# An encoder layer in emulated float32: 60 stores begun by GpSimd and 16 by ScalarE instead of SyncE

## The chip, the cores and the metric

The kernel runs on one core of a Trainium2 chip. Its time is device microseconds (us) of one execution, and of several runs the median is given. The engines are named as the profile names them: PE (TensorE, matrix products), DVE (VectorE), ACT (ScalarE), POOL (GpSimd) and SP (SyncE, which here only begins transfers). Each engine works through its own instructions in a fixed order. An instruction that begins a transfer (a DMA) stands in that order too: whatever it waits for, the instructions behind it on the same engine wait as well.

## The reference

One layer over 1024 frames of 1024 channels, all in float32. A product with `w_in` gives queries, keys, values, gates and merge logits. Branch A is a chunked gated linear attention, branch B a pooling mixer; the merged rows go through `w_out` and a layer norm.

```python
h = x @ w_in
q, k, v, gate_a, alpha_low, pool_in, gate_b, merge_logits = jnp.split(h, IN_OFFSETS, axis=-1)
...
y_a = o.reshape(B, S, GLA_DV).astype(x.dtype) * jax.nn.silu(gate_a)
y_b = _multiscale_pool(pool_in, w_pool_grp, pool_scale).astype(x.dtype) * jax.nn.silu(gate_b)
gates = jax.nn.sigmoid(merge_logits + b_merge)
g_a, g_b = jnp.split(gates, N_BRANCHES, axis=-1)
merged = g_a * (y_a @ w_proj_a) + g_b * (y_b @ w_proj_b)
y = merged @ w_out
return _layernorm(DEEPNORM_ALPHA * x + y, ln_g, ln_b)
```

## The kernel before

PE multiplies in float32 by parts: each operand is split into a high and a low part (L52, an ACT cast; L53, a DVE subtraction), and three products of the parts are summed.

Up to about 380 us the kernel loads `x`, projects, and runs the four attention heads; eight rows `la` (merge logits of branch A) are made in between by `la_gen`, copied by ACT and stored to DRAM (`la_d`, L295). From then on the work consists of pairs of output rows, each pair a 2 x 2 block product done with seven products instead of eight, of twelve matmuls each. The pairs, in order: `pi0..3` and `gb0..3` (branch B's input and gate), `gta0..3` (gate of branch A), `lb0..3` (merge logits of branch B), `pb0..3` (projection of branch B), `pa0..3` (projection of branch A, and the merge), `o0..3` (`w_out`).

Of a pair's seven weight blocks three are quarters of the raw weights (`raw_lb` and the like, L675) and four are sums of quarters, `S7`, `S6`, `S5`, `S3` (L614). POOL forms these sums for `pi`, `gb`, `gta` and `lb`, DVE for the later pairs. A product can't start before its sum has been formed and split.

The other operand of a product needs sums as well: four differences of its quarters, `T1..T4`. They are formed ahead of time: `Operands.ahead` loads four pieces (`xp`, `ybp`, `wop`, `yap`), POOL forms four 128x1024 differences (L196), and each is stored to DRAM (L198) and read back when its stage comes (L208). This is done twice for each of the operands X (at 29 to 56 us), YB (hooked to `gta0`, `gta1`), WO (`gta2`, `gta3`) and YA (`lb0`, `lb1`).

In `pb` and `pa` the product's rows are multiplied by a gate row (L835, L838/L839) and, in `pa`, added to the stored row of `pb` (L841). L839 and L841 run on POOL (in `pa3` on DVE). The results are stored by halves: `mb_d` (L851, 16 stores) and `m_d` (L855, 12 stores). The sigmoid rows of `lb` are stored to `gb_d` (L810, 8 stores) and read back as gates of `pb`.

All transfers of the kernel before, loads and stores, are begun by SP, on one hardware queue. A scheduler fixes each engine's order when the kernel is built, so moving a store to another engine also shifts other rows; the order is the same in every run.

Of the kernel before, what the change touches and what calls it, by code (L numbers as in the profile page):

```python
# [35 lines left out]
def encoder_layer(ctx: ExitStack, tc: tile.TileContext, xT, x, w_av, w_v, w_blk, w_up, b_al, g_norm,  # L36
                  w_pool, p_scale, b_mrg, w_pa, w_pb, w_o, ln_g, ln_b, ident_c, rcnt_c, masks_c, out):
    nc = tc.nc
    act, dve, pool_e, pe, sp = nc.scalar, nc.vector, nc.gpsimd, nc.tensor, nc.sync
# [73 lines left out]
    def w_in_gen(j, nm, then):  # L113

        w = load_split(w_blk[j], (KB, P), nm)
        ps = ps_acc.tile([P, S], F32, tag="acc", name=f"ps_{nm}")
        for half in range(2):
            i = 0
            for k in range(KB):
                hi, lo = w(k)  # L120
                for a, b in ((hi, xq[0]), (hi, xq[1]), (lo, xq[0])):
                    pe.matmul(ps[:, half * 512:half * 512 + 512], lhsT=a, rhs=mov(b, k, half), start=(i == 0), stop=(i == 23))  # L122
                    i += 1
                    yield 216
        then(ps)
# [58 lines left out]
    class Operands:  # L184
# [3 lines left out]
        def ahead(self, g, piece):  # L188

            q = {}  # L190
            for n in ("22", "12", "11", "21"):
                q[n] = piece(n, f"{self.nm}p{n}_{g}")
                self.fetch(q[n], n, g)
            for o, out_, a, b, op in (("T3", "22", "22", "12", ALU.subtract), ("T1", "12", "12", "11", ALU.subtract),
                                      ("T2", "11", "22", "11", ALU.add), ("T4", "21", "21", "11", ALU.subtract)):
                pool_e.tensor_tensor(out=q[out_], in0=q[a], in1=q[b], op=op)  # L196
                self.td[o, g] = dram.tile([P, 2, 512], F32, name=f"{self.nm}{o}_{g}d", tag=f"{self.nm}{o}_{g}d")
                sp.dma_start(self.td[o, g], q[out_])  # L198

        def make(self, o, pool):  # L200

# [50 lines left out]
    la_d = [dram.tile([P, S], F32, name=f"la_{j}", tag=f"la_{j}") for j in range(KB)]  # L252
# [38 lines left out]
    def la_gen(j, pool):  # L291
        def then(ps):
            s = pool.tile([P, S], F32, tag="sg", name=f"la_{j}")
            act.copy(s, ps)
            sp.dma_start(la_d[j], s)  # L295
        return w_in_gen(32 + j, f"la{j}", then)

    def ends(h):
# [275 lines left out]
    hs_ = (slice(0, 512), slice(512, 1024))  # L574

    def row(nm):
        return c4.tile([P, S], F32, tag="c", name=nm)
# [96 lines left out]
    def blk(w, j0):  # L674
        return lambda t, i: sp.dma_start(t.rearrange("p (a b) -> p a b", a=KB), w[j0 + i])  # L675
# [15 lines left out]
    def d_tile(nm):  # L691
        return dram.tile([P, S], F32, name=nm, tag=nm)

    yb_d, ya_d = Kept("yb"), Kept("ya")
    YB, YA = Operands("yb", yb_d.get), Operands("ya", ya_d.get)
    gb_d = [d_tile(f"gb_{j}") for j in range(KB)]
    mb_d = [d_tile(f"mb_{j}") for j in range(KB)]
    m_d = [dram.tile([P, 4, S], F32, name="m_0", tag="m_0"), dram.tile([P, 2, S], F32, name="m_1", tag="m_1")]
# [4 lines left out]
    def change(old, new):  # L703

        names = [p[1] for p in PRODUCTS]
        hooks = {0: [lambda: new.make("B11", op_a), lambda: new.make(names[1], old.pool[names[0]])]}
        for i in range(1, 6):
            hooks[i] = [lambda i=i: new.make(names[i + 1], old.pool[names[i]])]
        return hooks
# [80 lines left out]
    def y_a(j0):  # L790
# [10 lines left out]
        return then  # L801

    more = [ahead(YB, 0), ahead(YB, 1), ahead(WO, 0), ahead(WO, 1)]
    for q in range(4):
        items.append(gate_pair(f"gta{q}", 8 + 2 * q, AF.Silu, y_a(2 * q), hooks=more[q]))

    def keep(j0):
        def then(t):
            for i in range(2):
                sp.dma_start(gb_d[j0 + i], t(i))  # L810
        return then

    more = [ahead(YA, 0), ahead(YA, 1), None, change(X, YB)]
    for q in range(4):
        items.append(gate_pair(f"lb{q}", 40 + 2 * q, AF.Sigmoid, keep(2 * q), bias=8 + 2 * q, hooks=more[q]))


    def gated(nm, j0, operands, w, gate, more_d, out, hooks, eng):
        g, mb = {}, {}

        def get(i):
            if i not in g:
                g[i] = row(f"g{nm}_{i}")
                with tc.high_priority(offset=150):
                    gate(g[i], j0 + i)
                if more_d:
                    mb[i] = row(f"mb{nm}_{i}")
                    with tc.high_priority(offset=150):
                        sp.dma_start(mb[i], more_d[j0 + i])
            return g[i]  # L830

        def use(i, half, ps, more):
            o = get(i)[:, hs_[half]]
            if more is None:
                dve.tensor_tensor(out=o, in0=ps, in1=o, op=ALU.mult)  # L835
            else:
                t = post.tile([P, 512], F32, tag="t", name=f"t{nm}_{i}{half}", bufs=2)
                dve.tensor_tensor(out=t, in0=ps, in1=more, op=ALU.add)  # L838
                eng.tensor_tensor(out=o, in0=t, in1=o, op=ALU.mult)  # L839
            if more_d:  # L840
                eng.tensor_tensor(out=o, in0=o, in1=mb[i][:, hs_[half]], op=ALU.add)  # L841
            out(j0 + i, half, o)
        return Pair(nm, blk(w, j0), operands, use, hooks=hooks, s_eng=dve), get

    def gate_a(t, j):
# [2 lines left out]

    for q in range(4):
        items.append(gated(f"pb{q}", 2 * q, YB, w_pb, lambda t, j: sp.dma_start(t, gb_d[j]), None,  # L850
                           lambda j, half, o: sp.dma_start(mb_d[j][:, hs_[half]], o), change(YB, YA) if q == 3 else None, pool_e)[0])  # L851
    for q in range(4):
        def to_dram(j, half, o):
            if j < 6:
                sp.dma_start(m_d[j // 4][:, j % 4, hs_[half]], o)  # L855
        pair, m_last = gated(f"pa{q}", 2 * q, YA, w_pa, gate_a, mb_d, to_dram, change(YA, WO) if q == 3 else None,
                             dve if q == 3 else pool_e)
        items.append(pair)
# [136 lines left out]
```

## Time and profile before

| | us |
|---|---|
| median of 3 runs (1007.59 to 1009.13) | 1008.87 |
| the profiled execution | 1003.91 |
| its span in the trace | 1002.1 |
| PE busy in the span | 942.5 (94%) |
| DVE / ACT / POOL busy | 761.3 / 386.1 / 359.5 |
| moved by the one DMA queue | 163.59 MB |

The span is what the trace covers; the profiled execution is 1.8 us longer than its span and 4.96 us (0.5%) below the median of the runs. "PE" counts matmuls, "PEclk" is the clock that the throttle granted to PE as a share of full speed. A releaser ("<-") is the instruction whose end let a waiting instruction go.

### The profile page before, as it was taken

The numbers are of one execution on the slowest core, as the hardware profiler recorded it, in microseconds if no ns is written. First come the engines' busy times: TensorE is split into PE (matmuls) and PEld (weight loads), VectorE is DVE, ScalarE is ACT, GpSimd is POOL, SyncE is SP. The second block draws the span as 40 slices with busy tenths as digits, with TensorE's granted clock in tenths as the row PEclk, the third lists the DMA queues.
The fourth block names the chain that finished last, engine by engine and source line by source line (L and its number), as shares of the span: only waits on it lengthen the run. The fifth ranks groups of instructions, "written<-read, shape, count | busy, mean of one in ns | idle before, by whom it ended". The sixth has DMA issues, their size and how long they took to land. (4 is left out here: it accounts for less than half of the span.)

```text
span 1002.1 us, 13009 instructions
## 1 busy us (share of the span) xinstructions
PE 942.5 (94%) x4744; PEld 758.5 (76%) x4744; DVE 761.3 (76%) x1036; ACT 386.1 (39%) x625; POOL 359.5 (36%) x193
## 2 busy tenths in 40 slices
PE   9999799998999998999999999899999998989992
PEld 6887797886886885888888887678888876766871
DVE  5359959869666256857787778788886896689997
ACT  5255244253241225434333333233752552353330
POOL 1525323213213022322224267779111245510653
PEclk9999999999999999999999999999999999998997
DMA  8921120331123246121312498998987584496232
GB/s 274 348 85 34 40 74 22 76 111 42 44 91 84 85 121 230 43 95 53 118 52 94 136 331 305 325 330 325 385 287 250 215 323 162 165 302 200 102 120 84
DMA packets 72400, 164.41 MB, mean 164 GB/s; under 512 B 10208, under 2 KB 26848, under 8 KB 72336
## 3 DMA queue, kind: packets, MB, share of 16 engines
q1 hardware_dynamic: 72336, 163.59, 47.3%
q8 instruction: 37, 0.61, 0.3%
q14 instruction: 27, 0.22, 0.1%
HBM read 114.28 MB, written 49.28 MB: 163 GB/s over the span
## 5 line engine op out<-in xcount | busy, mean ns | idle before, releaser
L391 POOL TENSOR_TENSOR ks<-k,e 128x1024 f32<-128x1024 f32 x20 | 57.5, 2882 | 77.1 <-ACT e L387 67.5
L839 POOL TENSOR_TENSOR gpb<-tpb,gpb 128x512 f32<-128x512 f32 x12 | 21.6, 1799 | 87.5 <-DVE tpb L838 72.8
L122 PE MATMUL ps_la<-xh,wlo_la 128*128 128x512 f32 x128 | 51.4, 402 | 0.0
L122 PE MATMUL ps_la<-xl,whi_la 128*128 128x512 f32 x128 | 51.4, 401 | 0.0
L122 PE MATMUL ps_la<-xh,whi_la 128*128 128x512 f32 x128 | 51.0, 398 | 0.0
L387 ACT ACTIVATE e<-e 128x1024 f32<-128x1024 f32 x20 | 21.1, 1060 | 49.4 <-DVE e L386 49.3
L453 POOL TENSOR_TENSOR rsr_o<-rsa_o,mhalf 128x8 f32<-128x8 f32 x4 | 6.6, 1646 | 89.9 <-DVE rsa_o L452 89.9
L140 PE MATMUL ps_v<-whi_v,xh 128*128 128x264 f32 x128 | 37.4, 294 | 1.3 <-DVE k L288 1.3
L140 PE MATMUL ps_v<-whi_v,xl 128*128 128x264 f32 x128 | 37.5, 294 | 0.0
L444 DVE COPY v<-ps_o 128x256 f32<-128x256 f32 x32 | 13.4, 421 | 31.5 <-PE ps_o L441 25.6
L140 PE MATMUL ps_v<-wlo_v,xh 128*128 128x264 f32 x128 | 37.3, 294 | 0.0
L320 POOL TENSOR_TENSOR ke<-k,e 128x1024 f32<-128x1024 f32 x4 | 12.0, 3011 | 58.0 <-DVE k L288 28.6
L402 PEld LDWEIGHTS ps_s<-qs,ks 128*64 128x64 f32 x640 | 22.5, 140 | 13.7 <-issue 13.2
L390 DVE TENSOR_TENSOR qs<-q,e 128x1024 f32<-128x1024 f32 x20 | 30.2, 1512 | 3.2 <-ACT e L387 3.2
L614 POOL TENSOR_TENSOR S_gb<-raw_gb,raw_gb 128x512 f32<-128x512 f32 x4 | 6.3, 1587 | 67.1 <-DMA raw_gb<-in_w_blk 51.6
L402 PE MATMUL ps_s<-qs,ks 128*64 128x64 f32 x640 | 26.7, 229 | 3.3 <-DVE Pc L406 1.7
L122 PEld LDWEIGHTS ps_la<-xh,whi_la 128*128 128x128 f32 x128 | 24.2, 189 | 5.8 <-issue 0.4
L122 PEld LDWEIGHTS ps_la<-xl,whi_la 128*128 128x128 f32 x128 | 24.2, 189 | 5.4
L122 PEld LDWEIGHTS ps_la<-xh,wlo_la 128*128 128x128 f32 x128 | 24.2, 189 | 5.3
L196 POOL TENSOR_TENSOR ybp<-ybp,ybp 128x1024 f32<-128x1024 f32 x8 | 21.8, 2730 | 15.2 <-DMA ybp<-yb 10.6
L445 ACT ACTIVATE ps_o<-v 128x256 f32<-128x256 f32 x32 | 12.4, 387 | 37.5 <-DVE v L444 37.5
L122 PE MATMUL ps_k<-xl,whi_k 128*128 128x512 f32 x64 | 26.7, 417 | 0.0
(585 smaller groups left out, 3324.1 us busy)
## 6 DMA issues: line engine op xcount, KB each, us to landing
raw_v<-in_w_v SPq DMA_DIRECT2D x16, 264.0 KB, 2.7
xp<-in_xT SPq DMA_DIRECT2D x8, 512.0 KB, 6.7
oT<-oTs SPq DMA_DIRECT2D x32, 128.0 KB, 2.5
raw_la<-in_w_blk SPq DMA_DIRECT2D x8, 512.0 KB, 3.9
la<-la SPq DMA_DIRECT2D x8, 512.0 KB, 5.2
raw_pi<-in_w_blk SPq DMA_DIRECT2D x8, 512.0 KB, 4.3
raw_gb<-in_w_blk SPq DMA_DIRECT2D x8, 512.0 KB, 3.6
yb<-gb SPq DMA_DIRECT2D x16, 256.0 KB, 2.1
```

The costliest lines, as they stand in the source:

```text
L122: pe.matmul(ps[:, half * 512:half * 512 + 512], lhsT=a, rhs=mov(b, k, half), start=(i == 0), stop=(i == 23))
L140: pe.matmul(o, lhsT=sta(a, k, tb), rhs=w(k - k0)[b], start=(k == 0 and i == 0), stop=(k == KB - 1 and i == 2))
L196: pool_e.tensor_tensor(out=q[out_], in0=q[a], in1=q[b], op=op)
L320: pool_e.tensor_tensor(out=ke, in0=k, in1=e1, op=ALU.mult)
L387: act.activation(e, e, AF.Exp, scale=1.0 / TAU)
L390: dve.tensor_tensor(out=qs, in0=qt[h], in1=e, op=ALU.mult)
L391: pool_e.tensor_tensor(out=ks, in0=kt_[h], in1=e, op=ALU.mult)
L402: pe.matmul(psv[c * CH:c * CH + CH, b, :], lhsT=ks[:, cs], rhs=qs[:, cs], start=True, stop=True)
L444: dve.tensor_copy(v[b][:, hs], po)
L445: act.activation(po, v[b][:, hs], AF.Square, accum_out=d["ss"][:, b:b + 1])
L453: pool_e.tensor_tensor(out=r, in0=a, in1=mhalf[:, :w], op=ALU.pow)
L839: eng.tensor_tensor(out=o, in0=t, in1=o, op=ALU.mult)
```

## The change

76 stores are begun by another engine than SP: the 32 stores of differences (L198), the 16 of `mb` (L851) and the 12 of `m` (L855) by POOL, the 8 of `la` (L295) and the 8 of `gb` (L810) by ACT. Each stands in its new engine's order behind the instruction that makes its data, except that one half in four of `mb` is finished by DVE (L835): there POOL's store waits for DVE. The rows of `pa3` are stored neither before nor now. The number of bytes moved is the same. SP keeps all loads and the stores of `yb`, `ya` (L686), `oT` and `out`. SP's rows go from 377 to 302, POOL's from 198 to 258, ACT's from 590 to 606.

```diff
@@ Operands.ahead
                 pool_e.tensor_tensor(out=q[out_], in0=q[a], in1=q[b], op=op)
...
-                sp.dma_start(self.td[o, g], q[out_])
+                pool_e.dma_start(self.td[o, g], q[out_])
@@ la_gen
             act.copy(s, ps)
-            sp.dma_start(la_d[j], s)
+            act.dma_start(la_d[j], s)
@@ keep
-                sp.dma_start(gb_d[j0 + i], t(i))
+                act.dma_start(gb_d[j0 + i], t(i))
@@ gated
-            out(j0 + i, half, o)
+            out(j0 + i, half, o, pool_e if eng is pool_e else sp)
@@ pb
-                           lambda j, half, o: sp.dma_start(mb_d[j][:, hs_[half]], o), change(YB, YA) if q == 3 else None, pool_e)[0])
+                           lambda j, half, o, q: q.dma_start(mb_d[j][:, hs_[half]], o), change(YB, YA) if q == 3 else None, pool_e)[0])
@@ pa
-        def to_dram(j, half, o):
+        def to_dram(j, half, o, q):
             if j < 6:
-                sp.dma_start(m_d[j // 4][:, j % 4, hs_[half]], o)
+                q.dma_start(m_d[j // 4][:, j % 4, hs_[half]], o)
```

The first place is POOL's order around the weight sums of `lb1`, at some 657 to 680 us of the trace before. `S_lb_5538`, `5558`, `5580` and `5658` are S7, S6, S5 and S3 of `lb1`; `yap_0` are the four pieces of YA's first half. Before:

```order
L614 TENSOR_TENSOR S_lb_5538<-raw_lb_0_5344,raw_lb_1_5346 128x512
L614 TENSOR_TENSOR S_lb_5558<-raw_lb_1_5346,S_lb_5538 128x512
L614 TENSOR_TENSOR S_lb_5580<-raw_lb_1_5346 128x512
L614 TENSOR_TENSOR S_lb_5658<-raw_lb_0_5344,S_lb_5558 128x512
L196 TENSOR_TENSOR yap_0_5437<-yap_0_5437,yap_0_5439 128x1024
L196 TENSOR_TENSOR yap_0_5439<-yap_0_5439,yap_0_5441 128x1024
L196 TENSOR_TENSOR yap_0_5441<-yap_0_5437,yap_0_5441 128x1024
L196 TENSOR_TENSOR yap_0_5443<-yap_0_5443,yap_0_5441 128x1024
```

The same place of POOL's order in the changed kernel:

```order
L196 TENSOR_TENSOR yap_0_5437<-yap_0_5437,yap_0_5439 128x1024
L198 DMA yaT_0d<-yap_0_5437 128x1024
L196 TENSOR_TENSOR yap_0_5439<-yap_0_5439,yap_0_5441 128x1024
L198 DMA yaT_0d<-yap_0_5439 128x1024
L196 TENSOR_TENSOR yap_0_5441<-yap_0_5437,yap_0_5441 128x1024
L614 TENSOR_TENSOR S_lb_5538<-raw_lb_0_5344,raw_lb_1_5346 128x512
L198 DMA yaT_0d<-yap_0_5441 128x1024
L196 TENSOR_TENSOR yap_0_5443<-yap_0_5443,yap_0_5441 128x1024
L614 TENSOR_TENSOR S_lb_5558<-raw_lb_1_5346,S_lb_5538 128x512
L614 TENSOR_TENSOR S_lb_5580<-raw_lb_1_5346 128x512
L198 DMA yaT_0d<-yap_0_5443 128x1024
L614 TENSOR_TENSOR S_lb_5658<-raw_lb_0_5344,S_lb_5558 128x512
```

Three differences and two stores have moved ahead of S7 of `lb1`, and the fourth difference and the other two stores stand between its four sums. The orders around the sums of `gta2`, `lb0` and `lb2` change in the same way.

The second place is SP's order in the `pa` stage, at some 824 to 842 us, as one piece of the difference ("-" before, "+" after). `raw_pa_1_6865` is the second half of a pair's weights, `gpa` and `mbpa` are rows read for the merge, `m_3238` is where merged rows are stored.

```order
 L829 DMA mbpa_0_7047<-mb_3232 128x1024
-L855 DMA m_3238<-gpa_1_6853 128x512
-L855 DMA m_3238<-gpa_0_6883 128x512
-L855 DMA m_3238<-gpa_1_6853 128x512
 L846 DMA gpa_1_7175<-la_521 128x1024
+L675 DMA raw_pa_1_6865<-in_w_pa 128x1024
 L829 DMA mbpa_1_7178<-mb_3235 128x1024
-L675 DMA raw_pa_1_6865<-in_w_pa 128x1024
-L855 DMA m_3238<-gpa_0_6883 128x512
 L846 DMA gpa_0_7205<-la_520 128x1024
```

The weights' second half no longer stands behind three stores of merged rows, and it has changed places with the load of `mbpa`.

## Rows read from the trace of the kernel before

**Rows 1.** The page's first part: busy time, share of the span, instructions.

```profile
PE 942.5 (94%) x4744; PEld 758.5 (76%) x4744; DVE 761.3 (76%) x1036; ACT 386.1 (39%) x625; POOL 359.5 (36%) x193
```

**Rows 2.** Busy time by stretch (window: its length, each engine, PEclk, DMA share, GB/s).

```profile
575.00:600.00 25.00, 25.00 (x110) 20.27 (x109) 17.29 (x18) 9.48 (x16) 16.66 (x10) 1.00 0.89 314
600.00:625.00 25.00, 23.82 (x103) 18.86 (x102) 21.88 (x19) 9.95 (x17) 19.94 (x11) 1.00 0.81 305
625.00:650.00 25.00, 20.81 (x83) 16.43 (x82) 18.62 (x14) 6.64 (x12) 19.04 (x10) 0.93 0.93 330
650.00:675.00 25.00, 23.66 (x102) 18.93 (x101) 21.69 (x15) 10.38 (x16) 19.37 (x10) 1.00 0.94 344
675.00:700.00 25.00, 25.00 (x109) 20.23 (x108) 21.65 (x18) 8.62 (x14) 24.61 (x12) 1.00 0.85 306
```

**Rows 3.** Timeline of PE, matmuls that waited (start, duration, [idle before <-releaser]).

```profile
613.60 0.50 PE L635 MATMUL psa_gta<-xh,wlo_gta 128*128 128x512 f32 x1 [1.18 <-DVE wlo_gta L53]
...
640.01 0.71 PE L635 MATMUL psc_gta<-xT4h,whi_gta 128*128 128x512 f32 x1 [4.19 <-DVE e_gta L644]
...
844.45 0.47 PE L635 MATMUL psc_pa<-yaT4h,whi_pa 128*128 128x512 f32 x1 [3.15 <-DVE e_pa L644]
...
901.88 0.79 PE L635 MATMUL psc_o<-woT3h,whi_o 128*128 128x512 f32 x1 [4.32 <-ACT whi_o L52]
```

**Rows 4.** Busy time by stretch, behind the third of these waits.

```profile
844.90:848.30 3.40, 3.40 (x10) 2.63 (x9) 3.37 (x5) 0.40 (x1) 2.59 (x2) 0.50 0.00 1
```

**Rows 5.** Waits of SP's queue (line <- releaser: us in total, times, longest).

```profile
SPq L855 <- POOL gpa L841: 30.5, 8, 6.8
...
SPq L851 <- POOL gpb L839: 25.7, 10, 7.5
...
SPq L198 <- POOL ybp L196: 18.6, 7, 6.3
...
SPq L295 <- ACT la L294: 7.0, 1, 7.0
```

**Rows 6.** Groups by shape on POOL (busy us, mean ns of one | idle before).

```profile
L196 POOL TENSOR_TENSOR yap<-yap,yap 128x1024 f32<-128x1024 f32 x8 | 22.2, 2780 | 0.4
...
L841 POOL TENSOR_TENSOR gpa<-gpa,mbpa 128x512 f32<-128x512 f32 x12 | 19.6, 1644 | 0.7
...
L614 POOL TENSOR_TENSOR S_lb<-raw_lb,S_lb 128x512 f32<-128x512 f32 x8 | 11.4, 1429 | 6.9 <-DVE wlo_lb L53 6.6
...
L614 POOL TENSOR_TENSOR S_lb<-raw_lb,raw_lb 128x512 f32<-128x512 f32 x4 | 7.0, 1755 | 2.0 <-DMA raw_lb<-in_w_blk 2.0
...
L614 POOL TENSOR_TENSOR S_lb<-raw_lb 128x512 f32<-128x512 f32 x4 | 6.0, 1507 | 0.6 <-DVE wlo_lb L53 0.6
...
L453 POOL TENSOR_TENSOR rsr_ln<-rsa_ln,mhalf 128x1 f32<-128x1 f32 x8 | 4.9, 613 | 12.5 <-DVE rsa_ln L452 9.9 <-DVE rst_ln L456 2.6
```

**Rows 7.** Timeline of POOL, 657 to 684 us (a difference is wop or yap).

```profile
657.40 2.27 POOL L614 TENSOR_TENSOR S_lb<-raw_lb,raw_lb 128x512 f32<-128x512 f32 x1
659.74 1.63 POOL L614 TENSOR_TENSOR S_lb<-raw_lb,S_lb 128x512 f32<-128x512 f32 x1
...
667.88 1.29 POOL L614 TENSOR_TENSOR S_lb<-raw_lb,S_lb 128x512 f32<-128x512 f32 x1 [4.61 <-DVE wlo_lb L53]
669.12 14.11 POOL L196 TENSOR_TENSOR yap<-yap,yap 128x1024 f32<-128x1024 f32 x5
```

**Rows 8.** The chain that ended last, at the product of `lb1` with S7.

```profile
671.27 2.78 PE psc_lb L635 x12
```

**Rows 9.** Timeline of SP, 825 to 834 us (start, duration, what it begins).

```profile
825.14 6.14 SPq L855 DMA_DIRECT2D m<-gpa  x2
831.33 0.42 SPq L846 DMA_DIRECT2D gpa<-la  x1
833.38 0.32 SPq L829 DMA_DIRECT2D mbpa<-mb  x1
833.79 0.38 SPq L675 DMA_DIRECT2D raw_pa<-in_w_pa  x1
```

## The prediction, made before the changed kernel ran

> **What bounds the kernel now.** I read the page's busy times first: PE works in 94% of the span, and no other engine comes near [rows 1]. What can be won is therefore only time in which PE waits or runs at the lower clock, and what can be lost is new waiting of PE. Next I read the busy times in stretches of 25 us around the stage where POOL forms differences for three operands while it also forms the weight sums [rows 2]. PE is full in the first and the last of these stretches and lacks 1.18, 4.19 and 1.34 us in the three between; POOL lacks 8.34, 5.06, 5.96, 5.63 and 0.39 us of 25, together 25.4 us of 125. This is the only stage where POOL is nearly as full as PE, and it is where 24 of the 60 stores that POOL receives will be issued (YB's, WO's and YA's, eight each). Then the timeline of PE for its largest waits [rows 3]: each is released by DVE or ACT, which themselves follow a late load or a late row. The two larger ones behind 800 us are where SP's order matters. [...] Last, the waits of SP's queue [rows 5]: it stands 30.5 us for merged rows (L855), 25.7 for `mb` (L851), 18.6 for YB's differences and 7.0 for the one late `la` row, with later loads queued behind it.
>
> **What the change adds on POOL.** No transfer is begun by POOL in this trace, so its price there, d, is unknown. From below, the shortest arithmetic on POOL takes 0.61 us; from above, a 128x512 operation takes 1.64 [rows 6]. SP's own issues take 0.32 to 0.42 [rows 9], but I see no reason why POOL should match them, and use 0.61 as the low end. I take 1.0, as far from the one as from the other in ratio. Besides, an instruction that needs the result of the one ahead of it on POOL starts 0.07 us behind it (659.74 after 657.40 + 2.27) [rows 7], so a store costs 1.07.
>
> A pair of rows keeps PE busy for 7 products of 2.78, 19.46 us [rows 8]. In a pair with differences POOL does four of 2.78 (11.12) and four sums, 1.755 + 2 x 1.429 + 1.507 = 6.12, together 17.24 [rows 6], which leaves 2.22. Four stores at 1.07 are 4.28, so each such pair leaves POOL 2.06 us further behind. All 24 stores are 25.7 us, about the 25.4 that POOL has idle, and not all of that idle time can be used, since part of it waits for DVE, as the 4.61 us ahead of 667.88 do [rows 7].
>
> This alone would be absorbed, since sums are formed early. S7 of `lb1` ends at 659.67, PE needs its product at 671.27: a lead of 11.60 [rows 7, 8]. But the new order places three differences and two stores ahead of that S7: 3 x 2.78 + 2 x 1.07 = 10.48. The lead that is left is 1.12. POOL arrives there with the lateness of the three pairs `gta2`, `gta3` and `lb0`, 3 x 2.06 = 6.18, so S7 comes 6.18 - 1.12 = 5.06 late. The cover that hid POOL's work is then gone, and the rest of `lb1` and `lb2`, each with four stores, add 2.06 each, 4.12. Late sums make ACT's and DVE's splits late, and PE waits for these. One such wait will be long enough to be followed by the lower clock: 1.7 [rows 4]. **Loss: 5.06 + 4.12 + 1.7 = 10.9 us.** At d = 0.61 a pair is late by 0.50 and S7 isn't late (lead 1.9 against 1.5): about 1.0. At d = 1.64 a pair is late by 4.62, S7 by 14.0, and the loss is 14.0 + 9.2 + 1.7 = 25. Where the wait of 4.19 us at 640.01 stays, POOL catches up there; where DVE's new order removes it, PE gains as much. I count neither.
>
> The eight stores of X (29 to 56 us) and those of `mb` and `m` lie where POOL has room: it is busy for 36% of the span [rows 1]. I cost them at nothing; their cover is POOL's idle time, and if POOL became late in `pa`, its 12 rows would free `mbpa` later by one store each and the loads behind them too.
>
> [...]
>
> **What it gives on SP.** In `pa` SP stands until 831.28 for two stores of merged rows, and the weights' second half goes out at 833.79, behind the load of `mbpa` [rows 9]. In the new order it stands behind the load of `gpa` alone: 831.4 instead of 833.79, 2.4 us earlier. The wait at 844.45 becomes 3.15 - 2.4 = 0.75, short enough, as at 613.60, to be followed by no lower clock: gain 2.4 + 1.7 = 4.1. The wait of 4.32 at 901.88 follows `w_out` loads that stood behind merged rows in SP's queue; POOL's rows get later there too, so I take half, 2.2, between 0 and 4.32. The store of `la` that held SP for 7.0 us stood ahead of loads for `pi`; up to 1 us, counted in the low end alone. **Gain: 6.3 us,** at most 9.4.
>
> **What it adds on ACT.** Sixteen issues; by SP's rows 0.32 to 0.42 each [rows 9], at most 6.7 us on an engine that is busy for 39% [rows 1]. What hides them is ACT's idle time. If a `gb` store has to wait for an earlier transfer, the casts of weights queue behind it; I give that nothing in the sum.
>
> **Sum.** 10.9 - 6.3 = +4.6 us. The profiled execution took 1003.91, so 1008.5 for its like. It lies 4.96 below the median of the runs, and against that the same difference gives 1008.87 + 4.6 = 1013.5.
>
> **Rivals.**
> 1. *POOL has room after all.* If d is 0.6 or less, the loss is 1 us or none and SP's gain remains: -5.3 to -9.4, 1003.6 to 999.5. For it: 24 x 0.68 = 16.3 us against 25.4 idle. It decides from about d = 0.77 down: there a pair is late by 1.14, the lead left at S7 is 1.58, and the loss, 3 x 1.14 - 1.58 + 2 x 1.14 = 4.1 without a lower clock, is 2.2 below the gain. Against it: three differences ahead of a sum, whatever d is. 36%.
> 2. *Nothing to be seen.* The loads that go out earlier land no earlier, since the DMA engines are 81 to 94% busy at 575 to 700 us [rows 2], and POOL's lateness is covered by waits that PE has anyway (6.7 us in the three middle stretches). Both terms shrink to a few us: 1007 to 1011. 16%.
> 3. *Stores on POOL are dear.* If a store is held for as long as POOL's own operations beside DVE, d is 1.64, the loss 25 and the time 1008.87 + 18.7 = 1027.6. For it: DVE is busy 17 to 22 of 25 us there [rows 2]. 10%. [...]
>
> **Chances and range.** The forecast, a loss of a few us with d near 1, has 38%, and its own range is 1011 to 1019. A measurement of this kernel can tell about 0.2%, 2 us, from no change. Slower by more: forecast and third rival, 48%. Within: the second, 16%. Faster: the first, 36%. The range goes from the first rival's full gain, 999, to 1025, short of the dear case.
>
> **What would show it.** Right: POOL is full from 600 to 700 us; stores there take about 1 us of its order; PE waits for `wlo_lb` or `whi_lb` behind S7 at some 670 us; the wait at 844 shrinks to below 1 us without a lower clock. Wrong: PE as full at 600 to 700 us as before, POOL with idle time left (first rival), or a new wait of ACT on a `gb` store. What would make the sum wrong most easily is d, and next the loads: if YA's pieces land late, POOL waits for them ahead of S7, and the loss grows without any price of a store.

## The result, and the profile after

The changed kernel took 1029.60 us (median of 4 runs, 1025.02 to 1033.84) against 1008.27 for the kernel before on the same chip: ratio 1.0232 on record (the medians alone give 1.0212), 95% interval 1.0204 to 1.0261. It is slower by 21 us, beyond the predicted range. The profiled execution is the slowest of the four, 1033.84 us with a span of 1031.8, while that of the kernel before lay 4 to 5 us below its median. So the two spans differ by 29.7 us, and losses read from the two traces are together some 8 us larger than the 21 us of the medians.

Up to the pair `gta1` the two traces keep step: it starts at 581.15 us before and at 581.49 after. `lb3` starts at 707.29 and at 738.99. Of this stretch, 31.4 us longer, one row of the kernel before, by stretch as in [rows 2]:

```profile
581.15:707.29 126.14, 119.43 (x506) 95.65 (x504) 99.94 (x81) 45.78 (x74) 99.25 (x48) 0.99 0.90 329
```

and one of the changed kernel:

```profile
581.49:738.99 157.50, 131.64 (x506) 103.94 (x505) 109.70 (x81) 45.34 (x75) 100.26 (x71) 0.89 0.75 272
...
600.00:625.00 25.00, 20.82 (x79) 16.50 (x78) 19.04 (x15) 6.83 (x13) 14.06 (x11) 0.84 0.80 281
...
650.00:675.00 25.00, 19.97 (x77) 15.74 (x76) 21.04 (x13) 6.87 (x12) 15.78 (x12) 0.86 0.66 235
```

PE does the same 506 matmuls. It idles 157.50 - 131.64 = 25.86 us instead of 6.71, and the same work takes 12.2 us longer at a mean granted clock of 0.89 instead of 0.99. The last two rows answer to the second and fourth of [rows 2]: POOL, which the prediction saw full here, is busy for 14 and 16 of 25 us, less than before. The waits of PE that make up 21.7 of the 25.86 us, from the timeline of PE after (they answer to [rows 3]):

```profile
613.43 0.80 PE L635 MATMUL psc_gta<-xT3h,wlo_gta 128*128 128x512 f32 x1 [4.18 <-DVE wlo_gta L53]
...
639.40 0.79 PE L635 MATMUL psc_gta<-xT3h,wlo_gta 128*128 128x512 f32 x1 [4.09 <-DVE wlo_gta L53]
...
664.11 0.80 PE L635 MATMUL psa_lb<-xh,wlo_lb 128*128 128x512 f32 x1 [5.03 <-DVE wlo_lb L53]
...
693.49 0.79 PE L635 MATMUL psc_lb<-xT3h,wlo_lb 128*128 128x512 f32 x1 [3.00 <-DVE wlo_lb L53]
...
711.26 0.76 PE L635 MATMUL psc_lb<-xT4h,whi_lb 128*128 128x512 f32 x1 [5.36 <-DVE e_lb L644]
```

All five end with DVE. What DVE did is read from its timeline after:

```profile
605.19 8.18 DVE L53 TENSOR_TENSOR wlo_gta<-S_gta,whi_gta 128x512 fp32r<-128x512 f32 x1 [3.44 <-ACT whi_gta L52]
613.30 0.68 DVE L759 TENSOR_TENSOR gta<-psc_gta,u_gta 128x512 f32<-128x512 f32 x1
...
631.24 8.11 DVE L53 TENSOR_TENSOR wlo_gta<-S_gta,whi_gta 128x512 fp32r<-128x512 f32 x1 [1.21 <-ACT whi_gta L52]
...
651.72 12.33 DVE L53 TENSOR_TENSOR wlo_lb<-raw_lb,whi_lb 128x512 fp32r<-128x512 f32 x1
...
702.36 8.14 DVE L53 TENSOR_TENSOR wlo_lb<-S_lb,whi_lb 128x512 fp32r<-128x512 f32 x1
```

Each is one 128x512 subtraction. At 617.53 of the same trace, where POOL stands idle (615.33 to 623.51), one takes 0.68 us. The row behind the first, of the same size but with one operand in PSUM (`psc`), takes 0.68. Before, the longest 128x512 operation of this stage took 2.89 us, and the longest of all, twice as large, 3.43:

```profile
633.07 3.43 DVE L799 TENSOR_TENSOR gta<-oTl,gta 128x1024 f32<-128x1024 f32 x1
```

POOL's timeline after, over the first of these four:

```profile
603.21 1.29 POOL L614 TENSOR_TENSOR S_gta<-raw_gta,raw_gta 128x512 f32<-128x512 f32 x1 [2.02 <-DMA raw_gta<-in_w_blk]
604.45 0.58 POOL L198 DMA_DIRECT2D ybT_1d<-ybp  x1
605.05 2.41 POOL L196 TENSOR_TENSOR ybp<-ybp,ybp 128x1024 f32<-128x1024 f32 x1
607.40 1.30 POOL L614 TENSOR_TENSOR S_gta<-raw_gta,S_gta 128x512 f32<-128x512 f32 x1
608.66 1.27 POOL L614 TENSOR_TENSOR S_gta<-raw_gta 128x512 f32<-128x512 f32 x1
609.87 0.58 POOL L198 DMA_DIRECT2D ybT_1d<-ybp  x1
610.47 2.35 POOL L196 TENSOR_TENSOR ybp<-ybp,ybp 128x1024 f32<-128x1024 f32 x1
613.52 1.28 POOL L614 TENSOR_TENSOR S_gta<-raw_gta,S_gta 128x512 f32<-128x512 f32 x1 [0.70 <-DVE wlo_gta L53]
```

From 604.45 to 612.82 POOL never stands idle, and its operations are not slowed (2.41 us a difference; the mean of `yap` before was 2.78, [rows 6]). DVE's subtraction, begun at 605.19, ends at 613.37, 0.55 us after POOL's first pause begins; the other three end 0.55 to 0.56 us after the start of theirs. Beside the 0.68 us of one alone, I read this as DVE doing most of its work when POOL stopped. The `S7` that it splits had been formed by 604.50, in time for PE, which came to its product at 608.64:

```profile
608.64 0.39 PE L635 MATMUL psc_gta<-xT3h,whi_gta 128*128 128x512 f32 x1
```

So this PE wait isn't a late sum.

The price d of a store on POOL can now be read, from the groups by shape after:

```profile
L851 POOL DMA_DIRECT2D mb<-gpb x16 | 9.1, 571 | 4.0 <-POOL gpb L839 3.0 <-DVE gpb L835 0.6 <-DMA gpa<-la 0.3
...
L198 POOL DMA_DIRECT2D woT_0d<-wop x4 | 2.3, 577 | 0.3 <-POOL wop L196 0.3
```

It is 0.57 us, not 1.0. Where the store follows its own difference directly (626.23), POOL waits another 0.30 us ahead of it.

### The profile page after: what moved, and what is told of

Its sections match the earlier page's. It is cut to its first block, busy times and chain, and to the rows that moved or that the text cites. A ratio compares the mean times of both kernels' runs of the same rounds, so it can differ in the third digit from the quotient of the medians.

```text
span 1031.8 us, 13018 instructions
## 1 busy us (share of the span) xinstructions
PE 954.4 (92%) x4744; PEld 768.4 (74%) x4744; DVE 781.8 (76%) x1036; ACT 385.1 (37%) x625; POOL 376.1 (36%) x253
## 5 line engine op out<-in xcount | busy, mean ns | idle before, releaser
L53 DVE TENSOR_TENSOR wlo_gta<-S_gta,whi_gta 128x512 fp32r<-128x512 f32 x16 | 28.5, 1780 | 6.5 <-ACT whi_gta L52 6.5
L53 DVE TENSOR_TENSOR wlo_lb<-S_lb,whi_lb 128x512 fp32r<-128x512 f32 x16 | 22.2, 1408 | 8.5 <-ACT whi_lb L52 8.4
```

What stands on the lines that cost most here:

```text
L53: (lo_eng or dve).tensor_tensor(out=lo, in0=src, in1=hi.bitcast(F32), op=ALU.subtract)
```

## The experiments

Theory A: while POOL works without a pause, DVE's operations with two operands in SBUF don't get to run. Theory B, the prediction's: sums come late since differences and stores stand ahead of them. Theory C: the store itself is what shuts DVE out. A and C are guesses from the trace after, put to the runs; the "port" of the expectations is a name for what DVE waits for, and no run shows such a part. The runs were made in three groups, each compared with the kernel before on its own chip (medians 1005.31, 1003.94 and 1005.22); the ratios are those on record, which differ from the quotient of two medians by up to 0.2%. Stage is the stretch from the start of `gta1` to that of `lb3`, longest the longest DVE subtraction or product in SBUF at 560 to 740 us.

| run | ratio (interval) | stage us, PE busy, clock | longest us |
|---|---|---|---|
| before | 1 | 126.14, 119.43, 0.99 | 3.43 |
| changed | 1.0232 (1.0204 to 1.0261) | 157.50, 131.64, 0.89 | 12.33 |
| e1_diff_on_sp | 1.0000 (0.9985 to 1.0015) | 127.25, 119.72, 0.99 | 3.42 |
| e2_program_order | 1.0199 (1.0175 to 1.0224) | 133.90, 122.58, 0.96 | 3.93 |
| e3_order_only | 1.0056 (1.0032 to 1.0079) | 132.32, 122.90, 0.96 | 3.42 |
| e4_stores_old_order | 1.0082 (1.0057 to 1.0107) | 132.59, 121.17, 0.97 | 7.47 |
| f1_diff_only | 1.0295 (1.0270 to 1.0319) | 153.08, 129.83, 0.91 | 8.18 |
| f2_store_behind_difference | 1.0209 (1.0182 to 1.0235) | 144.95, 126.05, 0.94 | 5.83 |
| f3_small_transfers | 1.0150 (1.0125 to 1.0175) | 140.11, 125.81, 0.94 | 8.12 |
| f4_diff_on_act | 1.0034 (1.0016 to 1.0052) | 128.99, 121.20, 0.97 | 3.42 |
| g1_pair_with_wait | 1.0058 (1.0035 to 1.0080) | 133.86, 122.75, 0.97 | 3.42 |
| g2_pair_without_wait | 1.0258 (1.0223 to 1.0294) | 152.32, 126.09, 0.92 | 8.51 |
| g3_m_only | 0.9966 (0.9953 to 0.9978) | 127.33, 120.36, 0.97 | 3.42 |
| g4_act_only | 1.0005 (0.9988 to 1.0021) | 126.87, 119.42, 0.99 | 3.43 |

**e1_diff_on_sp**, the changed kernel with one line back:

```diff
-                pool_e.dma_start(self.td[o, g], q[out_])
+                sp.dma_start(self.td[o, g], q[out_])
```

> The changed kernel with its 32 stores of differences back on SP; stores of la and gb stay on ACT, of mb and m on POOL. POOL's order of sums and differences is the one of the kernel before. Theory A (held port: a DVE operation with two operands in SBUF can't start while POOL works without a gap, and the new order of POOL has no gaps): no DVE operation over 4 us at 575 to 725 us, none of the 31 us lost there; the gain at 844 us remains: 1000 to 1007. Theory B (late sums: the weight sums come late since differences and stores stand ahead of them): the same time, since both are gone. Theory D (the stores of gated rows or of gb cost something of their own): 1010 to 1020.

The whole loss is gone, so it came from the stores of differences; but the other 44 stores give nothing either.

**e2_program_order**, the changed kernel:

```diff
-                pool_e.tensor_tensor(out=q[out_], in0=q[a], in1=q[b], op=op)
+                tc.keep_in_program_order(pool_e.tensor_tensor(out=q[out_], in0=q[a], in1=q[b], op=op))
...
-                pool_e.dma_start(self.td[o, g], q[out_])
+                tc.keep_in_program_order(pool_e.dma_start(self.td[o, g], q[out_]))
...
+                if self.s_eng is pool_e:
+                    tc.keep_in_program_order(ins)
```

> The changed kernel with POOL's differences, their stores and the weight sums pinned in the order in which the program is written: each store right behind its own difference (POOL then stands 0.3 us for its own result, a gap), all four differences and stores of a half ahead of S3 of one pair and S7 of the next. Theory A: DVE gets its turn in each gap, no DVE operation over 4 us, 1003 to 1013. Theory B: each S7 now stands behind four differences and four stores instead of two or three and two: as slow as the changed kernel or slower, 1028 to 1040.

Each theory got one of its marks: no DVE operation over 4 us, as A said, and nearly the time that B said. The time goes to a place of its own, a single wait of PE of 10.78 us at 588.23 for `whi_gta`, since S3 of `gta0` had been put behind differences whose loads were late. That is B's mechanism, in an order that the changed kernel doesn't have. As a test between the two it was badly built.

**e3_order_only**, the kernel before, pinned at the end of building (`ORDER` is the list of differences and sums as the changed kernel has them, `PINS` their instructions):

```diff
+        for x, y in zip(ORDER, ORDER[1:]):
+            tc.add_manual_dep(PINS[y], PINS[x].name, mybir.DependencyInfo(
+                mybir.DependencyClass.NoSync, mybir.DependencyReason.DATA), reason="order")
```

> The kernel before, all stores on SP, with POOL's differences and weight sums pinned in the order of the changed kernel: no transfer is begun by POOL. Theory A in its plain form (the order has no gaps, with or without stores): DVE operations of 5 us and more at 600 to 710 us, 1015 to 1030. [...] Theory B: sums late by the moved differences alone, without 0.57 us per store: 1010 to 1018, with no long DVE operation.

The longest DVE operation is of 3.42 us: theory A in its plain form falls. C, which expects no hold where POOL begins no store, stands at 1009.93 us, and B's time is missed by only 0.1 us. POOL's timeline of this run at the same place (line numbers of the variants are a few higher):

```profile
604.62 1.27 POOL L621 TENSOR_TENSOR S_gta<-raw_gta,raw_gta 128x512 f32<-128x512 f32 x1
605.85 2.35 POOL L203 TENSOR_TENSOR ybp<-ybp,ybp 128x1024 f32<-128x1024 f32 x1
608.16 1.74 POOL L621 TENSOR_TENSOR S_gta<-raw_gta,S_gta 128x512 f32<-128x512 f32 x1
609.85 1.28 POOL L621 TENSOR_TENSOR S_gta<-raw_gta 128x512 f32<-128x512 f32 x1
```

and DVE's:

```profile
606.57 2.17 DVE L60 TENSOR_TENSOR wlo_gta<-S_gta,whi_gta 128x512 fp32r<-128x512 f32 x1 [6.01 <-ACT whi_gta L59]
```

POOL is as free of pauses here, yet DVE's subtraction, begun at 606.57, ends at 608.74, 0.54 us after the difference (608.20), and the sum begun at 608.16 takes 1.74 us, where the same sum takes 1.30 in the changed kernel (607.40). I read this as DVE getting its turn between two operations of POOL, with the sum waiting for it: without a transfer the two take turns here. The order alone costs 6.2 us in the stage, with no long DVE operation; that is the part of the loss that B can claim.

**e4_stores_old_order**, the changed kernel with the same added lines, and in `ORDER` the list as the kernel before has it, for instance:

```diff
-yap22_0 yap12_0 yap11_0 S7_lb1 yap21_0 S6_lb1 S5_lb1 S3_lb1
+S7_lb1 S6_lb1 S5_lb1 S3_lb1 yap22_0 yap12_0 yap11_0 yap21_0 yap22_1
```

> The changed kernel, stores of differences on POOL, with POOL's differences and weight sums pinned in the order of the kernel before; stores fall where the scheduler puts them, mostly right behind their own difference. Theory A: gaps are back, DVE operations up to 4 us, 1000 to 1010. Theory B: sums are early again, at most 0.57 us per store is left: 1002 to 1012. Theory C: long DVE operations stay, since all 24 stores do: 1018 to 1030.

Slower than A and B said by 3 and 1 us, faster than C. One DVE operation of 7.47 us remains, behind a store, a difference, a sum, a store and a difference without a pause. Together with e3 this asks for both: a store begun by POOL, and no pause behind it (theory A2).

**f1_diff_only**, the kernel before with one line of the change:

```diff
-                sp.dma_start(self.td[o, g], q[out_])
+                pool_e.dma_start(self.td[o, g], q[out_])
```

> The kernel before with only the 32 stores of differences begun by POOL; the stores of la, gb, mb and m stay on SP. If the whole loss comes from the differences, as the run with them back on SP says: 1.018 to 1.028 of the kernel before, DVE operations of 8 us and more at 600 to 710 us, and the wait of 3 us at some 844 us back. If the loss needs the other stores too: below 1.012.

The stores of differences alone make the loss, somewhat more of it than in the changed kernel and just above the 1.018 to 1.028 expected; the wait in `pa` is back, with 3.28 us at 871.04.

**f2_store_behind_difference**, the changed kernel, pinned as in e3, with each store named in the list behind its own difference:

```diff
-                pool_e.dma_start(self.td[o, g], q[out_])
+                PINS[f"{self.nm}p{out_}_{g}d"] = pool_e.dma_start(self.td[o, g], q[out_]).ins
```

> The changed kernel, order of POOL's differences and sums as it is there, with each store pinned right behind its own difference, where POOL stands 0.3 us for the result ahead of the store. Theory A2 (once POOL has begun a transfer, it keeps the port over the boundaries of back-to-back operations until it stands idle): runs without a gap are now at most a store, a sum or two and a difference, so no DVE operation over 6 us, 1.004 to 1.012 of the kernel before, against 1.023. Theory B (late sums and the price of the stores): order and stores are the same, 1.018 to 1.028.

The longest operation is 5.83 us, as A2 said; the time isn't: 1.0209 lies in B's range. PE idles for 144.95 - 126.05 = 18.9 us. Of this, 11.8 us are three waits of 3.5 to 4.4 us, each for a DVE subtraction of 4.6 to 5.8 us (ended at 634.68, 658.79 and 688.80) that would have been done before PE came, had it taken 0.68. So A2's mechanism is there, at a higher price than A2 gave it, and the time by itself doesn't decide between A2 and B.

**f3_small_transfers**, the kernel of e3 and, at the places of the stores:

```diff
+                if self.nm != "x":
+                    small = dram.tile([P, 8], F32, name=f"{self.nm}{o}_{g}s", tag=f"{self.nm}{o}_{g}s")
+                    PINS[f"{self.nm}p{out_}_{g}d"] = pool_e.dma_start(small, mhalf).ins
```

> The kernel pinned to the changed order with all its own stores on SP (1.0056 of the kernel before), to which POOL's order is added a transfer of 32 bytes per partition, from a constant to a place of its own in DRAM, at each of the 24 places where the changed kernel has a store of a difference; these transfers are extra. Theory A2: long DVE operations of 8 us and more come back and with them the loss, 1.015 to 1.030. Theory B or one in which the moved bytes matter: only 24 x 0.57 us of POOL's time, 1.005 to 1.012, no DVE operation over 4 us.

Against e3, 24 transfers of 32 bytes per partition bring DVE operations of 8.12 and 7.88 us back and 7.8 us of stage. So these holds didn't need the bytes of a store; it was enough that POOL began a transfer of 32 bytes per partition. But 7.8 us is less than a third of the 25.2 us between e3 and the changed kernel, and A2's range is only just reached: what the real stores do beyond this is not shown.

**f4_diff_on_act**, the changed kernel:

```diff
-                pool_e.dma_start(self.td[o, g], q[out_])
+                act.dma_start(self.td[o, g], q[out_])
```

> The changed kernel with its 32 stores of differences begun by ACT instead of POOL; POOL's order is nearly that of the kernel before. Theory A2: no DVE operation over 4 us. SP is free of these stores, but ACT now waits for POOL's results with casts of weights behind it: 0.995 to 1.010 of the kernel before; below 0.998 if SP's waits for differences had cost anything.

No hold (longest 3.42 us), and no gain from taking these stores off SP either (1.0034).

**g1_pair_with_wait** and **g2_pair_without_wait**, the changed kernel in its own order, pinned, with two tiny operations behind each store; g2 differs from g1 in the operand of the copy alone:

```diff
+                    PINS[f"{self.nm}p{out_}_{g}dm"] = pool_e.memset(small[:, :4], 0.0).ins
-                    PINS[f"{self.nm}p{out_}_{g}dc"] = pool_e.tensor_copy(small[:, 4:], small[:, :4]).ins
+                    PINS[f"{self.nm}p{out_}_{g}dc"] = pool_e.tensor_copy(small[:, 4:], mhalf[:, :4]).ins
```

> The changed kernel in its own order of POOL, with two tiny POOL operations behind each of the 24 stores of differences: a memset of 4 elements per partition and a copy of these, which has to wait for the memset (a wait of some 0.07 us). They add about 0.3 us of POOL's time per store, 7 us in all. Theory A2 (POOL keeps the port from a transfer on until it stands idle once): the wait ends the hold, so no DVE operation over 4 us, and 1.004 to 1.014 of the kernel before, faster than the changed kernel (1.023). Theory B (POOL's time): slower than the changed kernel, 1.025 to 1.035.

> As the run before, but the copy reads a constant, so it waits for nothing: the same two operations and the same time on POOL, no pause. Theory A2: DVE operations of 8 us and more remain, 1.020 to 1.035. If the mere presence of other operations behind a transfer ended the hold: no DVE operation over 4 us, and the time of the run before.

POOL's timeline of g2, with no pause, and DVE's behind it:

```profile
602.88 0.58 POOL L200 DMA_DIRECT2D ybT_1d<-ybp  x1
603.45 0.12 POOL L203 MEMSET ybT_1s<- 128x4 f32 x1
603.49 0.20 POOL L204 COPY ybT_1s<-mhalf 128x4 f32<-128x4 f32 x1
603.64 2.41 POOL L198 TENSOR_TENSOR ybp<-ybp,ybp 128x1024 f32<-128x1024 f32 x1
```

```profile
603.61 8.51 DVE L55 TENSOR_TENSOR wlo_gta<-S_gta,whi_gta 128x512 fp32r<-128x512 f32 x1 [4.20 <-ACT whi_gta L54]
```

and the same two of g1, where the copy starts 0.07 us after the memset's end:

```profile
607.79 0.58 POOL L200 DMA_DIRECT2D ybT_1d<-ybp  x1
608.36 0.12 POOL L203 MEMSET ybT_1s<- 128x4 f32 x1
608.55 0.72 POOL L204 COPY ybT_1s<-ybT_1s 128x4 f32<-128x4 f32 x1
609.23 2.84 POOL L198 TENSOR_TENSOR ybp<-ybp,ybp 128x1024 f32<-128x1024 f32 x1
```

```profile
606.62 2.60 DVE L55 TENSOR_TENSOR wlo_gta<-S_gta,whi_gta 128x512 fp32r<-128x512 f32 x2
609.14 0.68 DVE L55 TENSOR_TENSOR wlo_gta<-raw_gta,whi_gta 128x512 fp32r<-128x512 f32 x1
```

In g1 two subtractions of DVE, the first begun at 606.62, are done by 609.22, while the copy runs; it takes 0.72 us instead of g2's 0.20. I read this as DVE getting in at the pause and the copy waiting for it. From there to 615 us no operation of DVE takes over 3.42 us. A pause of 0.07 us per store, on an engine that has more to do, goes with 1.0258 - 1.0058 = 2.0%, 20 us. Both kernels have the same 24 stores and the same order of sums and differences, so for this larger part neither B nor C is left, and A2 is. The 20 us can't be put on the pause to the last one: the scheduler also placed some rows of DVE, ACT and SP differently in the two kernels.

**g3_m_only** is the kernel before with the first of these edits, **g4_act_only** with the other two:

```diff
-                sp.dma_start(m_d[j // 4][:, j % 4, hs_[half]], o)
+                pool_e.dma_start(m_d[j // 4][:, j % 4, hs_[half]], o)
...
-            sp.dma_start(la_d[j], s)
+            act.dma_start(la_d[j], s)
...
-                sp.dma_start(gb_d[j0 + i], t(i))
+                act.dma_start(gb_d[j0 + i], t(i))
```

> The kernel before with only the 12 stores of merged rows (L855) begun by POOL. If the 4.1 us gained at 844 us come from these stores leaving SP: the gain is there; it shows in the time, 0.994 to 0.998, if the loss in the o stage comes from the other stores, and not, 0.998 to 1.002, if merged rows land later by POOL and the first o pairs wait for them.

> The kernel before with only the 16 stores of la and gb begun by ACT. Nothing counted for them in the prediction: 0.997 to 1.003. If ACT's casts queue behind gb stores that wait for a transfer: above 1.003.

The timeline of PE in g3 at the wait that had been 3.15 us [rows 3]:

```profile
840.95 0.47 PE L635 MATMUL psc_pa<-yaT4h,whi_pa 128*128 128x512 f32 x1 [0.61 <-DVE e_pa L644]
```

Of all kernels g3 is the one that is faster than both, by 0.34%.

## Why the prediction was wrong

- **The step that failed** is the cost of the stores on POOL. It took a store for its time in POOL's order, and everything else on POOL and DVE for as long as before. The store's own price is 0.57 us, near the low end (0.61), at which the prediction had "about 1.0" of loss and the first rival a gain. The loss is there all the same: 31.4 us in the profiled stage, where the sum had 10.9. Of it, order alone is 6.2 (e3), order with stores and pauses is 7.7 (g1), and the remaining 23.7 goes with DVE operations of up to 12.33 us, the lower clock behind PE's waits for them included. The predicted direction was right for the wrong reason, which is luck.
- **POOL full, lateness per pair**: wrong. The stage has POOL busy for 100.26 of 157.50 us, and before `yap` it even waits 7.33 us for loads (at 677.27), the second thing that the prediction had named as able to make its sum wrong.
- **S7 of `lb1` late by 5.06 us**: right in kind and small. S7 ends at 687.52 and PE waits 1.19 us for its cast at 689.76; the sums of `gta2` and `gta3` were in time:

```profile
689.76 0.50 PE L635 MATMUL psc_lb<-xT3h,whi_lb 128*128 128x512 f32 x1 [1.19 <-ACT whi_lb L52]
```

- **One half-clock sequel, 1.7 us**: mis-sized. The 1.7 is half of the 3.40 us for which [rows 4] shows 0.50. In the stage after, PE's work took 12.2 us longer, beside seven waits of 1.19 to 5.36 us. In the 3.4 us behind those of 4.18, 4.09, 5.03 and 5.36 the granted clock was 0.50, behind those of 3.00 and 3.01 it was 0.53 and 0.71, and in the 3.0 us behind the one of 1.19 it was 1.00.
- **The gain at 844 us, 4.1 us**: the size came out at this place, in part by luck. The wait is 0.81 us after (875.38) with a granted clock of 1.00 in its stretch; in g3 0.61. The pair, `pa1`, takes 20.45 us instead of 24.44. But the weights' second half doesn't go out 2.4 us earlier. Counted from the start of its pair it goes out at 5.94 us (866.54 - 860.60) instead of 6.58 (833.79 - 827.21), and what released it was DVE's split of an earlier block. It lands 5.35 us later instead of 7.33; the load of `mbpa` now stands behind it. And the pair ahead, `pa0`, takes 2.2 us longer: PE waits 1.84 us at 843.22, with a granted clock of 0.75 from there to 850.00, where the kernel before had waits of 1.33 and 1.03 us at full clock. The two pairs together gain 1.8 us, not 4.1. PE's two waits after, and the load in the chain that ended last:

```profile
843.22 0.61 PE L635 MATMUL psc_pa<-yaT3h,wlo_pa 128*128 128x512 f32 x1 [1.84 <-DVE wlo_pa L53]
...
875.38 0.47 PE L635 MATMUL psc_pa<-yaT4h,whi_pa 128*128 128x512 f32 x1 [0.81 <-DVE e_pa L644]
```

```profile
866.54 5.35 DMA raw_pa<-in_w_pa
```

- **The gain in the o stage, 2.2 us**: wrong. The waits are 3.61 and 2.34 us (929.98, 933.54), where they were 4.32 and 1.45. Of the stores taken off SP, those of `m` give 0.34% alone (g3), and with those of `mb`, `la` and `gb` nothing is left of it (e1). Since `la` and `gb` alone change nothing (g4), the stores of `mb` cost by subtraction what `m` gains; that was not tried by itself.
- **SP's waits** changed place: the stores' waits for differences and gated rows [rows 5] are gone, and loads now wait for landings of earlier transfers; before, these waits came to 6.9 us at most for one such pair of line and transfer. SP's waits after:

```profile
SPq L208 <- DMA mb<-gpb: 17.0, 3, 12.6
SPq L796 <- DMA ya<-gta: 12.9, 4, 4.5
SPq L850 <- DMA mb<-gpb: 12.3, 1, 12.3
```

- **The third rival** had the right size (1027.6), by luck, and a store "held for as long as POOL's own operations beside DVE". What happened is the reverse: the stores take 0.57 to 0.61 us in the mean of every group, and DVE's operations are the long ones, up to 12.33 us. That a DVE operation and one of POOL can wait for each other without any transfer of POOL, I read from e3: a sum takes 1.74 us instead of 1.30 beside a subtraction of 2.17. That this lasts over many operations of POOL was seen only where POOL had begun a transfer: the longest DVE operation is of 3.42 us in e3, 8.12 in f3 and 12.33 in the changed kernel.

## What to carry to other kernels

Moving a store to GpSimd can cost more than its issue, here 31.4 us of one stage at 0.57 us a store: look at what VectorE does beside it. If VectorE has operations with two operands in SBUF on the path to TensorE, it is worth trying to keep GpSimd's transfers out of stretches where GpSimd works without a pause: with the stores of differences begun by SyncE or ScalarE (e1, f4) the longest such operation of the stage was 3.42 us, and with GpSimd 12.33. A real wait behind each transfer helped (g1, 0.07 us: 1.0058 against g2's 1.0258), but it still left 0.6%, where stores begun by SyncE left nothing (e1, 1.0000). And where a scheduler orders an engine's work, read the new order for pauses as well as for what stands ahead of what: in g1 the 0.07 us for which GpSimd waited for its own result behind a transfer were, as I read it, where VectorE got in.

## What the runs showed of the hardware

Counted over the traces of all fourteen kernels: at a boundary between two arithmetic operations of POOL (128x512 or larger) less than 0.05 us apart, with a DVE operation with two SBUF operands waiting, DVE got its turn in 371 of 371 cases where POOL had begun no transfer since its last pause, and in 1 of 49 where it had. In the changed kernel alone it was 0 of 11 where it had, and in the kernel before, where POOL begins none, DVE got its turn in every case. Behind a transfer a DVE operation took up to 12.33 us (the changed kernel), and up to 8.12 behind transfers of 32 bytes per partition (f3). With a pause of 0.07 us behind each store the longest was 3.42 (g1). It also ended at times at a further transfer: where POOL began another transfer while a DVE operation waited behind an earlier one, DVE got its turn in 11 of 28 cases, 7 of them in f3, and in 7 of the 11 no pause stood behind that transfer either. The 128x512 operations of this stage with one of their two operands in PSUM (L642, L644, L759) showed no such thing: each took 0.67 to 0.69 us in the kernel before and in the changed one. What POOL keeps from DVE, and why a transfer changes it, no run shows.
